# The opening of an encoder layer: the reciprocal root spread without a diagonal, `c` asked for first, chunk 0 by halves, the last squares summed apart, the sums of h held behind plain weights

## The chip, the core and the metric

The kernel runs on one core of a Trainium2 chip. A core has five engines that run their own instruction streams: TensorE (PE, whose weight loads are counted apart as PEld), VectorE (DVE), ScalarE (ACT), GpSimd (POOL) and SyncE (SP). DMA transfers are started from the queues of SP, ACT and POOL. The metric is the device time of one execution in microseconds; the time of a kernel is the median of its runs.

## What is computed

One layer of a bidirectional encoder, in float32, on 512 tokens of 1024 features. Its three blocks, a SwiGLU network, a pair of attention mixers and a second SwiGLU network, each read a normalised and modulated input, whose shift, scale and gate come from one vector `c`:

```python
c_act = silu(c)                                   # c (1024,)
mod = c_act @ w_mod + b_mod                       # w_mod (1024, 9 * 1024)
(sh1, sc1, g1, sh2, sc2, g2, sh3, sc3, g3) = split(mod, 9)

h = rmsnorm(x, norm_ffn1) * (1 + sc1) + sh1       # rmsnorm: x * rsqrt(mean(x*x, features) + EPS) * gain
x = x + 0.5 * g1 * swiglu(h, w_ffn1_in, w_ffn1_out)

h = rmsnorm(x, norm_mix) * (1 + sc2) + sh2        # then the two mixers, windowed and differential attention
x = x + g2 * (merged @ w_out)

h = rmsnorm(x, norm_ffn2) * (1 + sc3) + sh3
x = x + 0.5 * g3 * swiglu(h, w_ffn2_in, w_ffn2_out)
```

## The kernel before

Features lie on the 128 partitions, tokens on the free axis: `x` is eight tiles `x[0]` to `x[7]` of 128 features by 512 tokens, and "chunk k" is the features of `x[k]`. A product in float32 is made of three products of halves: a value is split into `high` (rounded by ACT) and `low` (value less high), and `w h` is taken as high·high + high·low + low·high. So each chunk of a weight matrix costs a load, a cast on ACT, a subtraction on DVE and three matmuls per output tile. `load_split` does it for the larger weights: line 211 loads `raw`, line 185 casts `high` on ACT, line 186 subtracts `low` on DVE; `mm3` (lines 174 to 176) issues the three matmuls.

A column of `mod` (128 features of a shift, scale or gate) is made by `mod_col`: a 128x1024 block of `w_mod` is loaded from SP's queue (512 KB), and DVE multiplies it with silu(c), which stands copied on all partitions, and sums along the row (line 272). For a scale, a second DVE operation on one column applies the norm's gain (line 279).

**The opening** stands in the order in which it is written (the scheduler leaves the order of all engines there):

1. ACT's queue loads `c` as one row, then `par` (all biases and gains); SP's queue loads `x[0]` to `x[7]`. Two matmuls of `ones` with the row spread `c` over the partitions (line 609). Eight filler matmuls on the identity follow (`warm`, line 615), whose output nobody reads.
2. SP's queue loads, for chunks 0 to 2, the scale's block, the first weights `w1s` (128x768) and the shift's block (`first_loads`).
3. The squares of `x` are taken on ACT, but on DVE for chunk 5, and added up on DVE (line 652). Eight matmuls with `ones` sum them over the features (line 337); DVE and POOL (line 308) make the reciprocal root, one value per token, tokens on partitions.
4. To have it along the free axis on every partition, DVE multiplies the identity with it to a `diagonal` (line 316), and a matmul of `ones` with the diagonal makes the `spread` (line 329). Fillers stand before and behind it.
5. The loop over the eight chunks. `hidden` makes chunk k of h: DVE x · scale · spread (line 346), ACT adds the shift and rounds `high` (line 347), ACT writes the value itself (line 350), DVE makes `low` (line 351). The weights of the chunk are split by `first_split` and `first_low`: for most chunks DVE subtracts (line 639), but for the chunks in `BY_DMA`, which are 1, 3, 5 and 7, ACT writes the negated high part (line 632) and a DMA of POOL's queue adds the weights to it in memory (line 633). Then 18 matmuls go into six banks (line 689):

```python
for w, h in ((wh, hh[k]), (wh, hl[k]), (wl, hh[k])):
    for i, out in enumerate(out1):
        PE.matmul(out, w[:, i * P : (i + 1) * P], h, start=first, stop=last)
```

**Behind the opening** three more rounds q = 3, 4, 5 of "plain" weights `w1i` follow, each with two weight blocks, 48 matmuls and `finish`; then the rest of the first network comes by "units", which multiply sums and differences of blocks of h with those of the weights. The sums and differences of h (`h_sum`: n1, n2, t3 and t4, each two operations on DVE at line 574 or 576 and two splits, lines 185 and 186) are made by calls that stand behind round 3 (n1, n2) and round 4 (t3, t4); here the scheduler places them on the engines by itself, as early as their operands allow.

**The two boundaries**, where `x` is complete and the next block's h is made, work by two halves of 256 tokens. Their order is written out too; each half takes its sums, root, diagonal and spread in the same way, while TensorE works on the other half's products. The call at the second boundary is at line 1762 and after; `x · scale · spread` is line 1717 there, and line 1123 is a transpose in the attention stage.

## Time and profile before

| | us |
|---|---|
| timed, median of 3 runs | 1063.11 |
| timed, lowest and highest | 1062.1, 1065.39 |
| the profiled execution, its own time | 1061.53 |
| the profiled execution, its span | 1059.8 |
| TensorE busy in the span | 1040.5 (98%) |
| DVE busy in the span | 794.8 (75%) |
| ACT busy in the span | 566.2 (53%) |
| mean granted TensorE clock | 0.997 of full speed |

The span runs from the first to the last recorded instruction; the rest of the execution's time, 1.7 us, lies around it. Rows of the profile give a line, an engine, an operation, `out<-in` by tile names, the shape, a count, and the busy time or the mean; a bracket like `[4.75 <-DVE sm L307]` says how long the engine had stood idle before the row and what ended that.

### The profile page before, as it was taken

What the parts mean: (1) busy time and instruction counts of PE and PEld (TensorE: products, weight loads), DVE (VectorE), ACT (ScalarE), POOL (GpSimd) and SP (SyncE); (2) the same over time, 40 slices, a digit from 0 to 9 for tenths busy, and PEclk for the clock granted to TensorE, in tenths of its full rate; (3) what the DMA queues carried; (4) which work ended last, traced back from release to release, by engine and by line L of the source; (5) the groups of instructions that cost most, each with busy time, mean ns of one, the idle gap of its engine ahead of it and who ended that gap; (6) DMA issues with size and microseconds to landing.
All of it is one profiled execution on the core that took longest, in us unless ns stands there. A gap on an engine that the chain in (4) does not pass through costs nothing.

```text
span 1059.8 us, 18652 instructions
## 1 busy us (share of the span) xinstructions
PE 1040.5 (98%) x7316; PEld 952.6 (90%) x7316; DVE 794.8 (75%) x1459; ACT 566.2 (53%) x928; POOL 154.9 (15%) x174
## 2 busy tenths in 40 slices
PE   7999999999999999999999999999999999999998
PEld 5789889899899998899778778989999999999997
DVE  7985667667796679859773587977889787867867
ACT  5564334344454352667765755534766546655553
POOL 1100010100110100443211101001111211112210
PEclk9999999999999999999999999999999999999999
DMA  9968687966974459695747843975498998988974
GB/s 340 365 208 201 209 212 190 265 158 203 281 184 152 165 199 410 217 269 126 180 92 186 225 148 101 371 224 118 97 232 195 222 230 215 222 221 214 214 151 125
DMA packets 69082, 220.91 MB, mean 208 GB/s; under 512 B 8193, under 2 KB 10881, under 8 KB 68994
## 3 DMA queue, kind: packets, MB, share of 16 engines
q1 hardware_dynamic: 46512, 146.52, 38.6%
q0 software_dynamic: 19488, 68.70, 35.2%
q10 hardware_dynamic: 2994, 4.51, 1.2%
q8 instruction: 57, 0.93, 0.3%
q14 instruction: 31, 0.25, 0.1%
HBM read 209.46 MB, written 10.23 MB: 207 GB/s over the span
## 4 chain that ended last, share of the span: by engine, by line
PE 78%; DVE 8%; issue 5%; ACT 5%; DMA 2%; POOL 1%; SPq 0%; ACTq 0%; DVEq 0%; POOLq 0%
PE acc L446 5%; PE acc L444 5%; PE acc L445 5%; PE sc L174 5%; PE sc L446 5%; PE sc L444 5%; PE sc L175 5%; PE sc L445 5%; PE sc L176 5%; PE acc L174 4%; PE acc L175 4%; PE acc L176 4%; PE acc L1045 2%; PE acc L1047 2%; PE acc L1046 2%
## 5 line engine op out<-in xcount | busy, mean ns | idle before, releaser
L185 ACT CAST high<-raw 128x1024 fp32r<-128x1024 f32 (+2 forms) x162 | 158.3, 986 | 166.6 <-PE acc L445 39.1
L186 DVE TENSOR_TENSOR low<-raw,high 128x1024 fp32r<-128x1024 f32 (+2 forms) x162 | 183.6, 1141 | 59.4 <-ACT high L185 58.5
L444 PE MATMUL acc<-b,high 128*128 128x256 f32 x508 | 141.0, 278 | 0.3 <-DVE f L523 0.3
L445 PE MATMUL acc<-b,high 128*128 128x256 f32 x508 | 140.6, 277 | 0.1
L446 PE MATMUL acc<-b,low 128*128 128x256 f32 x508 | 140.6, 277 | 0.0
L444 PE MATMUL sc<-b,high 128*128 128x256 f32 x500 | 138.4, 277 | 1.4 <-ACT f L521 1.4
L446 PE MATMUL sc<-b,low 128*128 128x256 f32 x500 | 138.5, 277 | 0.0
L445 PE MATMUL sc<-b,high 128*128 128x256 f32 x500 | 138.4, 277 | 0.0
L186 DVE TENSOR_TENSOR low<-u,high 128x1024 fp32r<-128x1024 f32 (+1 forms) x73 | 87.5, 1200 | 27.6 <-ACT high L185 26.2
L185 ACT CAST high<-u 128x1024 fp32r<-128x1024 f32 (+1 forms) x73 | 75.5, 1035 | 54.8 <-PE sc L175 16.0
L174 PE MATMUL sc<-b,high 128*128 128x512 f32 (+1 forms) x280 | 100.8, 360 | 0.0
L175 PE MATMUL sc<-b,high 128*128 128x512 f32 (+1 forms) x280 | 100.3, 358 | 0.0
L176 PE MATMUL sc<-b,low 128*128 128x512 f32 (+1 forms) x280 | 100.2, 358 | 0.0
L444 PEld LDWEIGHTS acc<-b,high 128*128 128x128 f32 x508 | 95.4, 188 | 0.8 <-DVE f L523 0.5
L445 PEld LDWEIGHTS acc<-b,high 128*128 128x128 f32 x508 | 95.5, 188 | 0.4 <-DVE b L1727 0.3
L446 PEld LDWEIGHTS acc<-b,low 128*128 128x128 f32 x508 | 95.4, 188 | 0.2 <-DVE low L186 0.2
L444 PEld LDWEIGHTS sc<-b,high 128*128 128x128 f32 x500 | 94.0, 188 | 1.6 <-ACT f L521 1.6
L446 PEld LDWEIGHTS sc<-b,low 128*128 128x128 f32 x500 | 93.9, 188 | 0.3 <-DVE low L186 0.2
L445 PEld LDWEIGHTS sc<-b,high 128*128 128x128 f32 x500 | 93.9, 188 | 0.0
L174 PE MATMUL acc<-b,high 128*128 128x512 f32 (+1 forms) x248 | 92.1, 371 | 0.2 <-DVE u L186 0.2
L176 PE MATMUL acc<-b,low 128*128 128x512 f32 (+1 forms) x248 | 90.2, 364 | 0.0
L175 PE MATMUL acc<-b,high 128*128 128x512 f32 (+1 forms) x248 | 90.1, 363 | 0.0
(369 smaller groups left out, 2675.4 us busy)
## 6 DMA issues: line engine op xcount, KB each, us to landing
u<-w_mod SPq DMA_DIRECT2D x40, 512.0 KB, 7.8
b<-w_mod SPq DMA_DIRECT2D x32, 512.0 KB, 6.0
raw<-w2i SPq DMA_DIRECT2D x31, 512.0 KB, 5.5
u<-w2i POOLq DMA_DIRECT2D x31, 512.0 KB, 7.0
u<-w1u POOLq DMA_DIRECT2D x24, 512.0 KB, 7.1
raw<-w1u SPq DMA_DIRECT2D x24, 512.0 KB, 6.8
raw<-w1o SPq DMA_DIRECT2D x24, 384.0 KB, 4.2
raw<-w_gate SPq DMA_DIRECT2D x16, 512.0 KB, 5.6
```

Of the source, the lines that this page charges most:

```text
L174: PE.matmul(out, wh, xh, start=first, stop=False)
L175: PE.matmul(out, wh, xl, start=False, stop=False)
L176: PE.matmul(out, wl, xh, start=False, stop=last)
L185: S.copy(hi, src)
L186: V.tensor_tensor(lo, src, f(hi), ALU.subtract)
L444: PE.matmul(out, wh[:, s], xh, start=first and j == 0, stop=False, skip_group_check=True)
L445: PE.matmul(out, wh[:, s], xl, start=False, stop=False, skip_group_check=True)
L446: PE.matmul(out, wl[:, s], xh, start=False, stop=last and j == 1, skip_group_check=True)
L1045: PE.matmul(out[t][:, 0:n], hh[k][:, ht], wh[:, o : o + n], start=k == 0, stop=False)
L1046: PE.matmul(out[t][:, 0:n], hh[k][:, ht], wl[:, o : o + n], start=False, stop=False)
L1047: PE.matmul(out[t][:, 0:n], hl[k][:, ht], wh[:, o : o + n], start=False, stop=k == NC - 1)
```

## The change

Nothing in the mathematics changes. In the opening:

- `c` is laid out as 128 rows of 8 values and is the first load of ACT's queue; eight matmuls of 128x128, the broadcast column with the identity, spread it over the partitions. The fillers are matmuls of 512 columns now: two before `c`'s, two behind, one on each of `x[4]`, `x[5]`, `x[6]`, one behind the sums and one behind the spread.
- All squares are taken on ACT. Chunk 7's are not added to the others but summed by a second group of eight matmuls into the same bank.
- `diagonal` is gone, here and at both boundaries. `spread` is one matmul for each 128 tokens, with the root's column, broadcast, as the weights and the identity as the moving operand. In the opening it stands behind the shift of chunk 0, and a small DVE copy of the root stands ahead of that.
- The shift's block of chunk 0 is loaded ahead of its weights `w1s`.
- Chunk 0 of h is made by halves of 256 tokens.
- The gain of the scale columns of chunks 1 to 7 is applied on ACT instead of at line 279 on DVE.
- Chunk 7 leaves `BY_DMA`; DVE makes its low weights in the loop's last turn.

Behind the opening, the plain weights of round q + 1 are asked for and split ahead of round q's products, behind the last splits issued before, and the sums of h are held (`issue_after`) behind splits of plain weights: n1 in round 3, the other three in round 5. `finish` is held in the same way.

The diff, with context cut; the tile `zero` of the attention stage, a small tile now, and the moved line of the tile `pos` are left out.

```diff
@@ -122,7 +122,7 @@
 LAST = 2
-BY_DMA = (1, 3, 5, 7)
+BY_DMA = (1, 3, 5)
@@ -182,10 +182,11 @@
     def split_from(hi, lo, src):
-        S.copy(hi, src)
-        V.tensor_tensor(lo, src, f(hi), ALU.subtract)
+        last = S.copy(hi, src), V.tensor_tensor(lo, src, f(hi), ALU.subtract)
+        split[:] = [i.ins for i in last]
+    split = []
     turn, holders = [0], {}
@@ -223,14 +224,8 @@
     make_identity(nc, ident)
-    crow = u4(F32).rearrange("p a b -> p (a b)")[0:1, :]
-    nc.scalar.dma_start(crow, a["c"].unsqueeze(0))
     par = keep([P, NPAR], "par")
     x = [xt() for _ in range(NC)]
-    nc.scalar.dma_start(par, a["par"])
-    for c in range(NC):
-        nc.sync.dma_start(x[c], a["x"][c])
@@ -264,7 +259,7 @@
         return begins[v]
-    def mod_col(v, c, w=None, in_order=False):
+    def mod_col(v, c, w=None, in_order=False, beside=False):
         if w is None:
@@ -276,7 +271,10 @@
             tc.keep_in_program_order(ins)
         if v in norms:
-            V.scalar_tensor_tensor(t, t, par[:, norms[v] + c : norms[v] + c + 1], b, ALU.mult, ALU.add)
+            if beside:
+                S.activation(t, t, AF.Identity, bias=b, scale=par[:, norms[v] + c : norms[v] + c + 1])
+            else:
+                V.scalar_tensor_tensor(t, t, par[:, norms[v] + c : norms[v] + c + 1], b, ALU.mult, ALU.add)
@@ -308,25 +306,16 @@
             return rs
-        def diagonal(self, rs, r=FULL[0]):
-            n = r.stop - r.start
-            nt = n // P
-            diag = f2()[:, 0:n]
-            V.tensor_tensor(
-                diag.rearrange("p (t q) -> p t q", t=nt),
-                ident.unsqueeze(1).broadcast_to([P, nt, P]),
-                rs.unsqueeze(2).broadcast_to([P, nt, P]),
-                ALU.mult,
-            )
-            return diag
-        def spread(self, diag, r=FULL[0]):
+        def spread(self, rs, r=FULL[0]):
...
             rb = self.st[r.start] if n < T else bank("op")
             rb = rb[:, T - n : T]
-            PE.matmul(rb, ones, diag, start=True, stop=True)
+            for t in range(n // P):
+                PE.matmul(
+                    rb[:, t * P : (t + 1) * P], rs[:, t : t + 1].broadcast_to([P, P]), ident,
+                    start=t == 0, stop=(t + 1) * P == n, skip_group_check=True,
+                )
             return rb
@@ -343,11 +332,17 @@
         t = f2()[:, r]
         s = modv[sh][:, c : c + 1]
+        if value is not None:
+            rb = rb[:, r]
         V.scalar_tensor_tensor(t, x[c][:, r], modv[sc][:, c : c + 1], rb, ALU.mult, ALU.mult)
...
         yield
         if value is not None:
-            S.activation(value, t.rearrange("p (t q) -> p t q", t=2), AF.Identity, bias=s)
+            if r.stop - r.start == T:
+                t3 = t.rearrange("p (t q) -> p t q", t=2)
+            else:
+                t3 = t.unsqueeze(1)
+            S.activation(value, t3, AF.Identity, bias=s)
         V.scalar_tensor_tensor(lo[:, r], t, s, f(hi[:, r]), ALU.add, ALU.subtract)
@@ -398,9 +393,9 @@
                     n += 1
                     if n == at[0]:
-                        diag = norm.diagonal(norm.close(ra), ra)
+                        rsa = norm.close(ra)
                     elif n == at[1]:
-                        ha = h_steps(norm.spread(diag, ra), ra)
+                        ha = h_steps(norm.spread(rsa, ra), ra)
                         run(ha, at[4])
@@ -408,10 +403,9 @@
             rs = norm.close(rb)
             run(ha, at[6])
-            diag = norm.diagonal(rs, rb)
             run(ha)
             run(steps, at[3])
-            hb = h_steps(norm.spread(diag, rb), rb)
+            hb = h_steps(norm.spread(rs, rb), rb)
             run(hb)
@@ -602,26 +596,41 @@
     cact = [sbuf("ka", [P, D], F32, 1)]
     hh, hl = new_h()
+    ccol = keep([P, 3 * NC], "ccol")[:, 0:NC]
+    nc.scalar.dma_start(ccol, a["c"])
+    tc.keep_in_program_order(nc.scalar.dma_start(par, a["par"]))
+    for c in range(NC):
+        nc.sync.dma_start(x[c], a["x"][c])
     with tc.manual_schedule(engines=BOUND | {mybir.EngineType.SP, mybir.EngineType.Pool}):
+        fill = bank("acc")
+        def warm(n, by=None):
+            if by is None:
+                by = ident.unsqueeze(1).broadcast_to([P, NT, P])
+            for i in range(n):
+                PE.matmul(fill, ident, by, start=True, stop=True)
+        warm(2)
         cb = [bank("sc") for i in range(2)]
-        for i in range(2):
-            PE.matmul(cb[i], ones[0:1, :], crow[:, i * T : (i + 1) * T], start=True, stop=True)
-        def warm(n):
-            out = bank("sc")[:, 0:P]
-            for i in range(n):
-                PE.matmul(out, ident, ident, start=True, stop=True)
-        warm(8)
-        w1 = {}
+        for n in range(NC):
+            i, j = n // 4, n % 4
+            PE.matmul(
+                cb[i][:, j * P : (j + 1) * P], ccol[:, n : n + 1].broadcast_to([P, P]), ident,
+                start=j == 0, stop=j == 3, skip_group_check=True,
+            )
+        warm(2)
+        w1, pos = {}, []
         def first_loads(k):
             scale = mod_load(SC1, k)
+            if k == 0:
+                pos.append(keep([P, NT], "pos", I32))
+            shift = mod_load(SH1, k) if k == 0 else None
             raw = sbuf("raw", [P, 1024], F32, RAW)
             nc.sync.dma_start(raw[:, 0:768], a["w1s"][k])
-            w1[k] = scale, mod_load(SH1, k), raw
+            w1[k] = scale, shift or mod_load(SH1, k), raw
@@ -644,24 +653,28 @@
         for c in range(NC):
             sq = f2()
-            if c == 5:
-                V.tensor_tensor(sq, x[c], x[c], ALU.mult)
-            else:
-                S.activation(sq, x[c], AF.Square)
-            if c:
+            S.activation(sq, x[c], AF.Square)
+            if c == NC - 1:
+                last = sq
+            elif c:
                 V.tensor_tensor(sq, sq, before, ALU.add)
...
                 for i in range(2):
                     S.activation(cact[0][:, i * T : (i + 1) * T], cb[i], AF.Silu)
-        n1.sums(sq, FULL[0], True, True)
+                warm(1, x[c + 1])
+            elif 4 < c < NC - 1:
+                warm(1, x[c])
+            if c == NC - 2:
+                n1.sums(sq, FULL[0], True, False)
+        n1.sums(last, FULL[0], False, True)
         mod_col(SC1, 0, w1[0][0])
         rs = n1.rstd(FULL[0])
-        warm(6)
-        diag = n1.diagonal(rs)
-        rb1 = n1.spread(diag)
-        warm(5)
+        warm(1)
+        V.tensor_copy(small(1), rs[:, 0:1])
         mod_col(SH1, 0, w1[0][1])
+        rb1 = n1.spread(rs)
+        warm(1)
         out1 = [b for _ in range(3) for b in pair_banks()]
@@ -670,18 +683,27 @@
                     hq[f"b{k // 4 + 1}{t + 1}"] = values[:, t * 1024 : (t + 1) * 1024]
                 values = values.rearrange("p (t k q) -> p t k q", t=2, k=4)
-            h1 = hidden(rb1, k, SC1, SH1, hh[k], hl[k], value=values[:, :, k % 4, :])
-            next(h1)
+            if k == 0:
+                h1 = [
+                    hidden(rb1, k, SC1, SH1, hh[k], hl[k], r, values[:, i : i + 1, k, :]) for i, r in enumerate(HALVES)
+                ]
+            else:
+                h1 = [hidden(rb1, k, SC1, SH1, hh[k], hl[k], value=values[:, :, k % 4, :])]
+            for h in h1:
+                next(h)
             if k + 3 < NC:
...
             if k == 0:
                 first_split(1)
+            elif k + 1 < NC:
+                mod_col(SC1, k + 1, w1[k + 1][0], beside=True)
+            for h in h1:
+                next(h)
+            if k == 0:
                 first_low(0)
-            elif k + 1 < NC:
-                mod_col(SC1, k + 1, w1[k + 1][0])
-            next(h1)
-            if k == 0:
-                mod_col(SC1, 1, w1[1][0])
+                mod_col(SC1, 1, w1[1][0], beside=True)
+            elif k == NC - 1:
+                first_low(k)
             wh, wl = w1.pop(k)[3:]
@@ -689,7 +711,8 @@
             if k + 1 < NC:
                 mod_col(SH1, k + 1, w1[k + 1][1])
-                first_low(k + 1)
+                if k + 2 < NC:
+                    first_low(k + 1)
             if k + 2 < NC:
@@ -835,22 +858,26 @@
         for q in range(3):
             finish(q, out1[2 * q : 2 * q + 2])
-        sums1 = ["n1", "n2", "t3", "t4"]
         units1 = {p: in_unit1(p) for p in range(PLAIN, NH)}
         for q in range(3, 2 * PLAIN):
-            w = loaded1 or [load_split(a["w1i"][q - 3, k], aside=ASIDE * (q == 5)) for k in range(2)]
-            loaded1 = None
+            w, sums_from = loaded1, split[1]
+            if q < 5:
+                with tc.issue_after(split[0]), tc.issue_after(split[1]):
+                    loaded1 = [load_split(a["w1i"][q - 2, k], aside=ASIDE * (q == 4)) for k in range(2)]
+            behind = split[1]
             out = pair_banks()
...
                     o = (k % 4) * 256 + i * P
                     mm3(out[i], wh[:, o : o + P], wl[:, o : o + P], hh[k], hl[k], k == 0, k == NC - 1)
-            for _ in range(2):
-                if sums1:
-                    h_sum(sums1.pop(0))
-            finish(q, out)
+            if q != 4:
+                with tc.issue_after(sums_from):
+                    for t in ("n1",) if q == 3 else ("n2", "t3", "t4"):
+                        h_sum(t)
+            with tc.issue_after(behind):
+                finish(q, out)
             if q == 3:
@@ -1759,10 +1786,10 @@
             if i == len(last) - 2:
                 run(steps, at[0])
-                diag = n3.diagonal(n3.close(T1), T1)
+                rsa = n3.close(T1)
             elif i == len(last) - 1:
                 run(steps, at[1])
-                ha = h_steps(n3.spread(diag, T1), 0)
+                ha = h_steps(n3.spread(rsa, T1), 0)
                 run(ha, at[4])
@@ -1773,11 +1800,10 @@
         for q in ("a12", "a22"):
             plain.prepare(q)
-        diag = n3.diagonal(rs, T2)
         run(ha)
         lead.prepare("a12")
         run(steps, at[3])
-        hb = h_steps(n3.spread(diag, T2), 1)
+        hb = h_steps(n3.spread(rs, T2), 1)
         run(hb, 3)
@@ -1880,7 +1906,7 @@
     o = {}
     o["x"] = con(n["x"].reshape(T, NC, P).transpose(1, 2, 0))
-    o["c"] = n["c"].reshape(D)
+    o["c"] = con(n["c"].reshape(NC, P).T)
     o["pos"] = con(n["positions"].reshape(NT, P).T)
```

More of the change, by code (lines that the diff above doesn't have):

```diff
@@ L700, in layer @@
     row = u4(F32).rearrange("p a b -> p (a b)")[:, 0:NROW]
-    pos = keep([P, NT], "pos", I32)
+    pos = pos[0]
     freq = keep([P, HD // 2], "freq")
@@ L1379, in start_a @@
         two = [v.rearrange("p (t k w d) -> p t k w d", t=NT, k=2, w=2) for v in two]
-        zero = keep([P, HD], "zero")
+        zero = small(1)
         V.memset(zero, 0.0)
```

## The prediction

> **What bounds the kernel now.** I read the page first, then busy time by stretches, then the chain of waits, then the timeline of the first 57 us.

> ```profile
> span 1059.8 us, 18652 instructions
> PE 1040.5 (98%) x7316; PEld 952.6 (90%) x7316; DVE 794.8 (75%) x1459; ACT 566.2 (53%) x928; POOL 154.9 (15%) x174
> ```

> TensorE is busy for 98% of the span. It idles for 1059.8 - 1040.5 = 19.3 us, and only that can be won. Stretches (columns: length, then busy time of PE, PEld, DVE, ACT, POOL, clock, DMA share, GB/s):

> ```profile
> 18.88:56.26 37.38, 34.94 (x145) 26.76 (x146) 37.17 (x64) 22.18 (x33) 4.35 (x5) 1.00 1.03 349
> 56.26:130.00 73.74, 73.74 (x444) 65.50 (x444) 50.09 (x68) 34.99 (x48) 6.06 (x7) 1.00 0.73 210
> ```

> From 18.88, where the first weight product starts, to 56.26, where the loop over the eight chunks has ended, DVE is busy for 37.17 of 37.38 us and the DMA engines are full. Afterwards TensorE has no idle time at all. So what the opening gains reaches the end, and the question is what the opening gains. Chain of waits (start, length, what):

> ```profile
> 17.99 0.95 DVE low L639
> ...
> 49.14 0.50 PE acc L689
> 49.63 0.23 PE sc L689
> ...
> 56.26 0.23 PE acc L174
> ```

> The chain runs along DVE from 18.0 until 49.1 (left out here: the same DVE lines over and over), then along 29 matmuls, (56.26 - 49.63)/29 = 0.228 us each. A chunk has 18 of them, 4.10 us; eight need 32.8 us, and the loop takes 37.4: 4.6 us are open to the change.

> **Ahead of the loop.**

> ```profile
> 1.02 0.29 POOL masks.py:199 TENSOR_SCALAR_AFFINE_SELECT ident<-ident 128x128 f32<-128x128 f32 x1
> 2.90 3.75 PE L609 MATMUL sc<-u,ones 1*128 1x512 f32 x4 [2.90 <-DMA u<-c]
> par<-par ACTq DMA_DIRECT2D x1, 48.5 KB, 3.2
> 6.58 3.55 PE L615 MATMUL sc<-ident 128*128 128x128 f32 x16
> 9.95 2.28 DVE L652 TENSOR_TENSOR f<-f,f 128x512 f32<-128x512 f32 x3
> 12.29 1.09 PE L337 MATMUL tp<-ones,f 128*128 128x2 f32 x8 [2.15 <-DVE f L652]
> 13.79 1.04 POOL L308 TENSOR_TENSOR sm<-sm,half 128x4 f32<-128x4 f32 x1 [4.75 <-DVE sm L307]
> 14.86 0.69 DVE L316 TENSOR_TENSOR f<-ident,sm 128x512 f32<-128x512 f32 x1 [1.16 <-POOL sm L308]
> 15.94 1.35 PE L329 MATMUL op<-f,ones 128*128 128x512 f32 x2
> 17.12 1.28 PE L615 MATMUL sc<-ident 128*128 128x128 f32 x10
> 17.32 0.75 DVE L346 SCALAR_TENSOR_TENSOR f<-x,mod,op 128x512 f32<-128x512 f32 x1 [0.57 <-PE op L329]
> 18.88 0.50 PE L689 MATMUL acc<-b,high 128*128 128x512 f32 x1 [0.48 <-ACT b L347]
> ```

> The sum of squares of chunk 5 moves from DVE to ACT and chunk 7's is no longer added. Two DVE operations go, and the last add ends near 10.6 instead of 12.2. But `c`, now in 128 short rows, lies behind two filler matmuls, and three more that read x stand ahead of the sums. `c` came at 2.9 in one row; `par`, of 128 rows, took 3.2 us. Asked for within the first microsecond, `c` is there between 2.9 and 4.2. The first two fillers need only the identity, which is done at 1.3; at half clock they last from 1.4 to 4.8 and hide `c`. The L615 rows show 8 and 5 matmuls as x16 and x10, two passes each; a 128-column pass takes 0.21 us at half clock (x16, less the end of the last) and 0.11 at full (x10). Seven 512-column matmuls (eight such passes each) and eight 128-column ones (two each) are 72 passes: 15.1 us at half clock, 7.9 at full. Full clock came here no later than the end of the first L615 run, 3.55 us after its start, since the sums behind it (x8) took 0.14 us a pass or less. So I take it between 1.4 + 3.4 = 4.8 and twice that time from the start, 8.2. The sums then start at 8.4 + half of that: 10.8 to 12.5. Two groups of sums of 0.9 us end at 12.6 to 14.3, against 13.4 now: nothing sure is won here.

> From there to the reciprocal root is the same 1.45 us (13.38 to 14.83). Then the diagonal's DVE operation (0.6) goes, the spread is four pairs of passes (0.9 at full clock) beside the shift column on DVE (1.3), and chunk 0 is made in halves (ACT can start on the first half when DVE has done at least half of the 0.75, so it is up to 0.3 earlier). The first product comes 2.75 us after the root instead of 4.05: at 16.8 to 18.5, from 18.88. Call it t0.

> **Inside the loop.**

> ```profile
> 26.06 0.95 DVE L639 TENSOR_TENSOR low<-raw,high 128x768 fp32r<-128x768 f32 x1
> 26.93 0.74 DVE L346 SCALAR_TENSOR_TENSOR f<-x,mod,op 128x512 f32<-128x512 f32 x1
> 27.59 1.21 DVE L272 CUSTOM_DVE_ANT_0 u<-u,ka 128x1024 f32<-128x1024 f32 x1
> 28.73 0.68 DVE L576 TENSOR_TENSOR b<-b 128x512 f32<-128x512 f32 x1
> 29.33 0.21 DVE L279 SCALAR_TENSOR_TENSOR mod<-mod,par,begin 128x1 f32<-128x1 f32 x1
> 29.46 0.74 DVE L351 SCALAR_TENSOR_TENSOR b<-f,mod,b 128x512 fp32r<-128x512 f32 x1
> 30.13 1.27 DVE L272 CUSTOM_DVE_ANT_0 u<-u,ka,par 128x1024 f32<-128x1024 f32 x1
> ```

> Start to start, one chunk costs DVE 0.66 + 1.14 + 0.66 + 1.20 = 3.66 us, and 0.87 more where DVE makes the low weights. Four operations of the sums of h (0.60 each, 2.4) leave the loop, and seven L279 (0.13 or more each, 0.9) go to ACT, which is busy for 22 of these 37 us. What is left on DVE is 4.10 us a chunk in the mean, as much as TensorE needs. By DVE alone the loop would end at t0 + 4.8 (from chunk 0 to chunk 1, below) + 7 x 4.10 = t0 + 33.5. Two other things end later.

> ```profile
> 20.61 0.91 POOL L633 DMA_DIRECT2D low<-w1s  x1 [5.78 <-ACT low L632]
> 23.69 0.50 PE L689 MATMUL acc<-b,high 128*128 128x512 f32 x1 [0.39 <-ACT b L347]
> 28.01 0.50 PE L689 MATMUL acc<-b,low 128*128 128x512 f32 x1 [1.30 <-DMA low<-w1s]
> 34.65 0.84 ACT L630 CAST high<-raw 128x768 fp32r<-128x768 f32 x1 [1.21 <-DMA raw<-w1s]
> 35.39 0.84 ACT L632 ACTIVATE low<-raw 128x768 fp32r<-128x768 f32 x1
> 36.52 0.86 POOL L633 DMA_DIRECT2D low<-w1s  x1 [9.63 <-ACT low L632]
> DMA to landing us min/median/max: 7.4/7.8/8.7
> ```

> Chunk 1's low weights are asked for 1.7 us after the first product and land 9.1 after it; TensorE wants them at about t0 + 7.6 (18.88 to 23.69 is 4.8 to chunk 1, then 12 matmuls) and stops for 1.3 us now. Everything in this moves with t0, so the stop stays and chunk 2 begins near t0 + 10.5.

> Chunk 5's low weights do not move with t0. ACT had waited until 34.65 for the raw weights, which lie in a stream that keeps the DMA engines full from the start; no byte ahead of them is taken away. So ACT is done at 36.2, the accumulating DMA is issued at 36.5 and lands 7.8 later, at 44.3. TensorE would want it at t0 + 10.5 + 3 x 4.10 + 2.7 = t0 + 25.5, at 42.3 to 44.0: earlier. It waits, and then has 6 + 18 + 18 = 42 matmuls, 9.6 us. The loop ends at 53.9 instead of 56.3: **2.4 us**, almost whatever t0 is. That chunk 7's transfer goes (DVE does it instead, 0.87, beside chunk 7's products) frees the stream only behind this point.

> [...]

> **Behind the loop.** All sums of h (sixteen such operations, at 0.60 each 9.6 us) now stand behind the splits of plain weights. On DVE, weight splits queue behind them, and TensorE's first unit waits for both; DVE's idle 73.74 - 50.09 = 23.7 us cover it. Without that cover up to 9.6 us of sums would stop TensorE. The two boundaries lose a diagonal per half:

> ```profile
> 740.45 0.42 DVE L316 TENSOR_TENSOR f<-ident,sm 128x256 f32<-128x256 f32 x1
> 740.78 0.47 DVE L1717 SCALAR_TENSOR_TENSOR b<-x,mod,tp 128x256 f32<-128x256 f32 x1
> 740.92 0.70 PE L329 MATMUL op<-f,ones 128*128 128x256 f32 x2 [0.50 <-DVE f L316]
> PE tp L1123 <- DVE u L186: 2.0, 5, 0.8
> ```

> At the second boundary the 0.50 goes, but the operations of h behind it, which TensorE waits for next, come only 0.33 earlier (740.45 to 740.78): 0.3 us won. At the first boundary no wait names the diagonal: nothing. The spread itself has as many passes as before. The built program also orders some transposes and products of the attention stage anew. The five waits at L1123 bound that: 2.0 us won to 2.0 lost. I take 0.

> **Sum.** 2.4 + 0.3 = 2.7 us: the profiled execution goes from 1061.53 to 1058.8. The timed runs are 1062.1, 1063.11 and 1065.39; the median of all four is 1062.6, so I expect 1059.9.

> **Rivals.** *The stream does not hold chunk 5* (0.23): if ACT gets the raw weights or the DMA lands 1.5 us sooner, the loop ends by chunk 1's stop, at t0 + 10.5 + 6 x 4.10 = t0 + 35.1, 51.9 to 53.6. At 52.5, in the middle, 3.8 us are won, with the boundary 4.1: 1058.5; where chunk 1's stop shrinks too (1.3), 1057.2. For it: landing ranges over 7.4 to 8.7, and with DVE ahead the stream may be asked for earlier. Against: it is full already.

> *Given back* (0.12): the attention stage's new order loses the 2.0 us, and the time is 1061.9, no measurable change. For it: five waits stand there now. Against: DVE has less to do.

> *The fillers run cold* (0.11, slower): if full clock does not come before the sums, these start at 1.4 + 15.1 = 16.5 and end at 20.0 (sixteen passes); 1.45 to the root, 1.7 for the spread at half clock and 1.4 to the first product put t0 at 24.5. Then chunk 5 is wanted at 50.0 and the loop ends at 59.6, 3.3 us later: 1065.6. It decides from t0 = 21.2, where t0 + 25.5 is 2.4 past 44.3. For it: the x16 row is cold although TensorE had been busy since 2.9. Against: that was one-row work (1x512), and 3.55 us of 128-row work ended it.
> [...]

> **How the numbers follow.** The forecast has 0.54, its own range 1058.5 to 1061.5. About 0.3% (3.2 us, below 1059.9) is what a measurement of this kernel can tell. Faster: the first rival and a little over half of the forecast, 0.54. Slower: the last rival and 0.01, 0.12. The rest, 0.34, is within. The range goes from 1056.2 (first rival with 1 of the 2.0 us won) to 1063.2.

> **What would show it.** Right: a second wait of TensorE for `low<-w1s`, between 42 and 44.3, the first product of plain weights near 53.9, and a spread at the second boundary that waits for nothing. Wrong: no such wait, or the loop ending before 52.5; TensorE stopping for sums of h between 75 and 100; passes of 0.21 us still at 12.

## The result: slower by 0.24%

The changed kernel takes 1066.21 us in the median of 13 runs (1063.56 to 1068.76), the kernel before 1063.11 us in 13 runs beside it. The ratio is 1.0024, with a 95% interval of 1.0012 to 1.0035. Forecast were 1059.9 us and a range that ended at 1063.2. One run of the experiments, of e3_wrap, was slow, 1733.55 us, and is counted in no figure below.

The profiled execution of the changed kernel took 1068.76 us, the slowest of its 13; sizes read from it may be too large, and the medians are used where a total is wanted. Its page:

```profile
span 1067.0 us, 18682 instructions
PE 1047.6 (98%) x7330; PEld 957.1 (90%) x7330; DVE 792.1 (74%) x1449; ACT 569.3 (53%) x937; POOL 154.0 (14%) x173
```

TensorE's idle time is 1067.0 - 1047.6 = 19.4 us, as before (19.3). What grew by 7 us is the time in which it counts as busy, and the page alone does not say where. So the same matmul was looked up in both traces, stage by stage, and the difference of its two start times taken (changed less before; each number is the difference of two rows):

| at (us, before) | stage | difference |
|---|---|---|
| 18.9 | first product of chunk 0 | -1.7 |
| 72 to 172 | plain weights, first units | -2.9 |
| 369 to 511 | first boundary, projections | -1.5 to -1.4 |
| 525 to 540 | gates and attention | between +4.9 and +7.0 |
| 566 to 735 | mixers, up to the second boundary | +4.7 to +5.0 |
| 768 to 805 | behind the second boundary | +6.1 |
| 834 to the end | second network | +6.7 |

The opening does what was forecast: it wins 2.9 us, and these reach 172 us untouched. 1.4 us go between 172 and 369 us; most of the loss, 6.2 us, is made between 511 and 525, in a stage whose text the diff does not touch. The three largest waits of TensorE in the changed kernel (us in total, times, longest):

```profile
PE acc L176 <- DMA low<-w_gate: 3.6, 1, 3.6
PE acc L711 <- ACT b L338: 1.5, 2, 0.8
PE tp L1150 <- DVE u L185: 1.4, 3, 0.9
```

The first line has no counterpart before: a product of a gate's weights waits 3.6 us for the low weights that a DMA of GpSimd adds up. Around it (columns as in the prediction's stretches; the third number from the end is the granted clock):

```profile
524.26:527.67 3.41, 1.24 (x6) 0.64 (x6) 2.17 (x9) 2.79 (x12) 0.00 (x0) 1.00 0.85 160
527.67:531.08 3.41, 1.97 (x5) 1.58 (x6) 1.39 (x4) 1.49 (x2) 1.97 (x2) 0.50 0.37 76
531.08:534.49 3.41, 3.41 (x10) 2.64 (x9) 0.00 (x0) 0.00 (x0) 0.00 (x0) 0.50 0.88 203
746.13:749.54 3.41, 1.89 (x14) 1.49 (x13) 2.12 (x5) 1.69 (x4) 0.00 (x0) 1.00 0.69 253
```

The wait, which ends at 529.1, is paid twice: while it lasts, and in half a clock that is granted for 6.8 us, from 527.7 to 534.5. A product of the gate takes 0.43 us from start to start there and 0.23 at full clock; 13 of them lose 2.6 us. That time is booked as busy. The wait itself is idle time: this stage (511 to 545 us before) has 2.9 us more of it and the opening 3.4 less, which is why the idle time did not grow. The last line belongs to the second boundary, below.

The opening itself, in the timeline of the changed kernel:

```profile
11.26 1.84 PE L326 MATMUL tp<-ones,f 128*128 128x2 f32 x16
13.40 1.04 POOL L306 TENSOR_TENSOR sm<-sm,half 128x4 f32<-128x4 f32 x1 [4.23 <-DVE sm L305]
14.49 1.16 PE L315 MATMUL op<-ident,sm 128*128 128x128 f32 x8 [0.42 <-POOL sm L306]
17.21 0.50 PE L711 MATMUL acc<-b,high 128*128 128x512 f32 x1 [0.70 <-ACT b L338]
26.28 0.50 PE L711 MATMUL acc<-b,low 128*128 128x512 f32 x1 [0.90 <-DMA low<-w1s]
43.51 0.50 PE L711 MATMUL acc<-b,low 128*128 128x512 f32 x1 [0.42 <-DMA low<-w1s]
53.18 0.39 PE L174 MATMUL acc<-b,high 128*128 128x512 f32 x1
```

Sums at 11.3, first product at 17.2, a stop for chunk 1's low weights, one for chunk 5's at 43.5, and the first product of plain weights at 53.2 (56.1 before).

### The profile page after: what moved, and what is told of

Same layout as the page of the kernel before. It is cut to its first block, busy times and chain, and to the rows that moved or that the text cites. A ratio compares the mean times of both kernels' runs of the same rounds, so it can differ in the third digit from the quotient of the medians.

```text
span 1067.0 us, 18682 instructions
## 1 busy us (share of the span) xinstructions
PE 1047.6 (98%) x7330; PEld 957.1 (90%) x7330; DVE 792.1 (74%) x1449; ACT 569.3 (53%) x937; POOL 154.0 (14%) x173
## 4 chain that ended last, share of the span: by engine, by line
PE 75%; issue 9%; DMA 5%; DVE 5%; ACT 4%; POOL 2%; ACTq 0%; POOLq 0%; DVEq 0%; SPq 0%
PE sc L174 5%; PE sc L176 5%; PE sc L175 5%; PE sc L438 5%; PE sc L440 5%; PE sc L439 4%; PE acc L176 4%; PE acc L174 4%; PE acc L175 4%; PE acc L438 4%; PE acc L440 4%; PE acc L439 4%; PE acc L1072 2%; PE acc L1074 2%; PE acc L1073 2%
## 5 line engine op out<-in xcount | busy, mean ns | idle before, releaser
L174 PE MATMUL sc<-b,high 128*128 128x512 f32 (+1 forms) x280 | 100.6, 359 | 0.0
L174 PE MATMUL acc<-b,high 128*128 128x512 f32 (+1 forms) x248 | 93.1, 376 | 0.0
```

The source lines that it names most:

```text
L174: PE.matmul(out, wh, xh, start=first, stop=False)
```

## Experiments: where the 6 us behind 500 us come from

In the built program the order of instructions differs from that of before in two places outside the edited code: matmuls 3191 to 3319 of TensorE (the gates and the attention, 518 to 542 us before) and 4177 to 4247 (the mixers' end, 680 to 689). Neither the opening, nor the boundaries, nor the holding of the sums moves them: with all of these in place, the program of e1_slot, below, has the old order. One line does, and e2_before_early_ask, where it alone is moved, has the new order in both places: the call that asks for round 5's plain weights now stands ahead of round 4's products, and so ahead of the preparation of the first unit's weights `s1`.

That call also takes a buffer. High and low weights live in five places of one long tile, handed out in turn by `high_low`, and a place held by a unit is skipped:

```python
i = turn[0] % HILO            # HILO = 5
turn[0] += 1
i = i * 1024 + aside          # aside: 0 to 64 columns
return tuple(t[:, i : i + n] for t in parts)
```

Before, `s1` got place 2 and round 5's weights 3 and 4; now the weights get 2 and 3 and `s1` gets 4. From the third place handed out after these on, every place is one lower (0 becomes 4) to the end of the kernel. The turn would not matter if the places were alike. They are not: weights that are set 16 columns `aside` reach 16 columns into the next place, and only place 4 has nothing behind it. In the attention stage gate 5 (j = 5) is set aside and gate 6 is not. Before, they had places 4 and 0, which share nothing. Now they have 3 and 4, which share 16 columns, and gate 6's split must wait until gate 5's products have been made. The transfers that add up the gates' low weights show it (line of the kernel before, then of the changed one, grouped between 470 and 530 us: count, issue in ns, start of the first and the last):

```profile
L986 POOL DMA_DIRECT2D low<-w_gate x6: 862/898/909, 476.8 to 522.9; - x6
```

```profile
L1013 POOL DMA_DIRECT2D low<-w_gate x6: 865/899/930, 475.6 to 529.6; - x6
```

The first, gate 5's, starts 1.2 us earlier than before, the sixth 6.7 us later. From gate 6 on, each comes one turn late: gate 6's starts at 498.6, where gate 7's started at 500.0 before, and gate 6's at 488.9.

Theory: this order of places costs the time. Rivals: the new opening, the held sums or the new spread make the later stages late.

**e1_slot**, the changed kernel with the places handed out as before:

```diff
+                if q == 4:
+                    slot = turn[0]
+                    turn[0] += 1
                 with tc.issue_after(split[0]), tc.issue_after(split[1]):
                     loaded1 = ...
...
+                later_slot, turn[0] = turn[0], slot
                 units1[PLAIN].prepare("s1")
+                turn[0] = later_slot
```

> The changed kernel with one thing taken back: round 5's plain weights are still asked for ahead of round 4's products, but the high and low buffers are handed out in the order of the kernel before. Theory (the order of the buffers costs the time): the opening's 2.9 us stay and all that was lost behind 100 us comes back, so about 1060.2, and TensorE's 3.6 us wait for low<-w_gate near 529 us is gone. Rival (something in the new opening, the held sums or the spread at the boundaries makes later stages late): as the changed kernel, about 1066.

Measured: 1059.74 us (12 runs), ratio to before 0.9971 [0.9959, 0.9982]. The wait for `low<-w_gate` is gone, and the attention stage has full clock:

```profile
500.00:560.00 60.00, 58.06 (x352) 46.47 (x351) 43.34 (x118) 44.49 (x103) 13.13 (x13) 1.00 0.57 139
```

The theory holds, the rivals fall: 6.5 us hang on the places that are handed out (by the two ratios 0.53%, 5.6 us).

**e2_before_early_ask**, the other way round: the kernel before with that call alone moved.

```diff
             loaded1 = None
+            if q == 4:
+                loaded1 = [load_split(a["w1i"][2, k], aside=ASIDE) for k in range(2)]
```

> The kernel before with one thing of the change alone: round 5's plain weights are asked for ahead of round 4's products, which moves the handing out of high and low buffers by one place for the rest of the kernel. Opening, sums of h and boundaries are as before. Theory: the whole later loss without the opening's gain, about 1069 (1066.2 + 2.9), with a wait of some 3 us for low<-w_gate near 525 to 530 us. Rival: no change, 1063.

Measured: 1070.63 us, ratio 1.0070 [1.0055, 1.0085]: 7.4 us lost without any of the opening. The same wait appears:

```profile
PE acc L176 <- DMA low<-w_gate: 3.8, 1, 3.8
```

**e3_wrap**, the changed kernel, places as changed, but gate 6 set aside too, so that the step from aside to not aside falls on the wrap from place 4 to place 0 again.

```diff
-            wh, wl = load_main(a["w_gate"][j], ASIDE * (j == EARLY_A))
+            wh, wl = load_main(a["w_gate"][j], ASIDE * (j in (EARLY_A, EARLY_A + 1)))
```

> The changed kernel, in which one more gate (j = 6 besides j = 5) has its weights set 16 columns aside. If what costs the time in the attention stage is that gate 5 (16 columns aside, buffer 3) and gate 6 (not aside, buffer 4) share 16 columns, so that gate 6's split must wait for gate 5's products, then this lifts it: about 4 to 6 us below the changed kernel, 1060.5 to 1062, and no wait for low<-w_gate near 529 us. If the addresses alone matter, or the opening, about 1066.

Measured: 1060.93 us (11 runs), ratio 0.9977 [0.9967, 0.9988]. The attention stage's order is that of before again, and there is no wait for `low<-w_gate`. 5.3 of the 6.5 us are back; the rest, 1.2 us, lies within the two intervals.

**e9_before_gate5_not_aside**, the kernel before with gate 5 moved by 16 columns and nothing else:

```diff
-            wh, wl = load_main(a["w_gate"][j], ASIDE * (j == EARLY_A))
+            wh, wl = load_main(a["w_gate"][j], 0)
```

> The kernel before with one thing changed: gate 5's weights are not set 16 columns aside, so that they share 16 columns with the last weights of the projections ahead (buffer 3, aside) instead of beginning at the wrap from buffer 4 to buffer 0. Nothing else moves, no buffer is handed out in another order. Theory (16 shared columns make a split wait for the products of the buffer beside it, and the loads of the attention stage then come one turn late): slower by 3 to 7 us, 1066 to 1070, with waits of TensorE for low<-w_gate between 470 and 550 us. Rival (the turn of the buffers as such, or their addresses, cost the time): 1062.5 to 1063.5.

Measured: 1072.42 us, ratio 1.0081 [1.0068, 1.0093]: 9.1 us lost, more than expected.

```profile
PE acc L176 <- DMA low<-w_gate: 2.5, 1, 2.5
PE acc L174 <- ACT high L984: 1.5, 1, 1.5
```

No place is handed out in another order here, and no opening is new. Sixteen shared columns are enough.

## Experiments: what each part is worth

**e4_free_sums**: the changed kernel with the block of plain weights and sums of h of the kernel before.

```diff
-            w, sums_from = loaded1, split[1]
-            if q < 5:
-                with tc.issue_after(split[0]), tc.issue_after(split[1]):
-                    loaded1 = ...
+            w = loaded1 or [load_split(a["w1i"][q - 3, k], aside=ASIDE * (q == 5)) for k in range(2)]
+            loaded1 = None
...
+            for _ in range(2):
+                if sums1:
+                    h_sum(sums1.pop(0))
+            finish(q, out)
```

> The changed kernel with the plain weights and the sums of h as in the kernel before (not held, asked for in their own rounds); opening and boundaries changed. The buffers then are those of before too. Theory: no later loss, but four operations of the sums, 2.4 us of VectorE, back in the loop: 1060.5 to 1062.6, loop over the chunks ending up to 2.4 us later than the changed kernel's 53.35. If the held sums give nothing because the loop is held by something else: 1060.2, loop end at 53.4. Rival (opening or boundaries cause the loss): 1066.

Measured: 1062.43 us, ratio 0.9991 [0.9981, 1.0002]. The loop ends at 53.9, only 0.7 behind the changed kernel. Three operations of the sums, not four, stand in it (at 35.4, 47.3 and 47.9), and they cost it little: the profiles of e1_slot, e3_wrap and e8_diagonals, which have the changed kernel's opening and loop, end it between 52.7 and 53.8. But then:

```profile
66.03 0.50 PE L174 MATMUL acc<-b,high 128*128 128x512 f32 x1 [1.11 <-ACT high L185]
```

Round 4's weights come 1.1 us late, and between 62 and 68 us 1.9 more are lost against the changed kernel. The loop had ended 2.2 us sooner than before, and its next reader was not ready: most of the opening's gain is given back here unless the weights are asked for a round ahead.

**e5_sums_free_early_ask**: e1_slot with the weights asked for ahead, but the sums not held.

```diff
-            if q != 4:
-                with tc.issue_after(sums_from):
-                    for t in ("n1",) if q == 3 else ("n2", "t3", "t4"):
-                        h_sum(t)
+            if q < 5:
+                for t in ("n1", "n2") if q == 3 else ("t3", "t4"):
+                    h_sum(t)
```

> As e1_slot, but the four sums of h are not held: n1 and n2 stand behind round 3 and t3 and t4 behind round 4 as before, and the scheduler puts four of their operations back into the loop over the chunks. The plain weights are still asked for one round ahead. If what the block of plain weights gains over e4_free_sums (2.7 us) is VectorE's relief in the loop, as the prediction had it, this gives it up: 1061.5 to 1062.5. If it is the weights asked for early (in e4_free_sums TensorE waits 1.1 us at 66.0 for the cast of round 4's weights), it keeps it: 1059.5 to 1060.3.

Measured: 1067.46 us, ratio 1.0040 [1.0026, 1.0055]. Neither expectation. Up to 91 us it runs 0.3 to 0.4 us behind e1_slot, loop end 53.0: the three operations of the sums in the loop cost nothing that could be told. Then the first unit's weights are late. SP's queue, which loads them, waits for a column of `mod` (line 267) that stands on VectorE behind the sums, 23.5 us against 13.2 in e1_slot, and the loads go out ten us later (e1_slot, then e5_sums_free_early_ask):

```profile
66.16 0.38 SPq L472 DMA_DIRECT2D raw<-w1u  x1
76.60 0.38 SPq L472 DMA_DIRECT2D raw<-w1u  x1
```

ScalarE then sits idle for 7.7 us, until 92.4, for a transfer of these weights, and TensorE stops:

```profile
94.93 0.58 PE L438 MATMUL tp<-b,high 128*128 128x256 f32 x1 [3.27 <-ACT high L185]
96.50 0.58 PE L440 MATMUL tp<-b,low 128*128 128x256 f32 x1 [0.77 <-DVE low L185]
```

4.0 us of waits, and half a clock granted from 94.2 to 101.0. Asking early without holding the sums loses more than it gains (holding them without asking early was not run), and what the holding saves is at 95 us, not in the loop.

**e6_block_alone**: the kernel before with that block (asked early, sums held, places as before). Its diff is the block's part of the change, with e1_slot's lines.

> The kernel before with the block of plain weights alone (asked for one round ahead, sums of h held), buffers handed out in the order of before; opening and boundaries as before. If the loop is bound by VectorE, four operations less (2.4 us) end it near 54 in place of 56.3, and this has most of the gain without a new opening: about 1061. If opening and block only pay together, 1062.8 to 1063.5.

Measured: 1060.89 us, ratio 0.9986 [0.9973, 0.9998]. With the old opening four operations less on VectorE do end the loop earlier, at 54.4 for 56.1. From its first product it lasts 35.4 us; in the three profiles with the old loop and sums (before, e2_before_early_ask, e9_before_gate5_not_aside) it lasts 37.2.

**e11_loop_with_old_head**: e6_block_alone, and in the loop line 279 on ScalarE for chunks 1 to 7 and chunk 7 out of `BY_DMA`.

```diff
-BY_DMA = (1, 3, 5, 7)
+BY_DMA = (1, 3, 5)
...
-                mod_col(SC1, k + 1, w1[k + 1][0])
+                mod_col(SC1, k + 1, w1[k + 1][0], beside=True)
```

> As e6_block_alone (opening ahead of the loop as before: fillers, c as a row, diagonal, chunk 0 whole), with the change's loop: line 279 on ScalarE for chunks 1 to 7 and chunk 7's low weights by VectorE. The prediction said that the loop ends near 53.9 almost whatever the start of the first product is, held by chunk 5's transfer. Then about 1060, near e1_slot. If TensorE's own pace from the first product holds it (18.9 + 32.8 + stops of 2.3 = 54.0 to 54.5), it is 0.7 to 1.4 behind e1_slot: 1060.4 to 1061.1.

Measured: 1061.52 us, ratio 0.9983 [0.9969, 0.9997]; first product at 19.46, loop end at 55.3. No wait for chunk 5's low weights shows; the loop ends some 36 us behind the first product, with 2.3 us of stop for chunk 1's. The loop's own changes gain nothing here: e6_block_alone, without them, ended it at 54.4.

**e12_l279_on_vector**: e1_slot without `beside=True`.

> As e1_slot, but the gain of the scale columns is applied on VectorE (line 279) again. By the prediction's sum that puts 0.9 us back on VectorE in the loop: if VectorE binds there, 1060.3 to 1060.7; if TensorE's pace does, 1059.5 to 1060.0.

Measured: 1059.96 us, ratio 0.9965 [0.9953, 0.9977]. Moving line 279 to ScalarE is worth nothing that can be measured.

**e7_dma_1_3** and **e10_dma_3**: e1_slot with `BY_DMA = (1, 3)` and with `BY_DMA = (3,)`.

> As e1_slot, but chunk 5's low weights too are made by VectorE and not by the accumulating DMA. The prediction held that this transfer ends the loop; then the wait for low<-w1s near 43.5 goes and VectorE's rate takes over (0.87 more): loop end within 0.5 of e1_slot's 52.8 on either side, 1059.2 to 1060.3. If VectorE has no room in the loop, its 0.87 and more shows as waits for b<-f L351 or low<-raw: 1060.6 or more.

> As e1_slot, but VectorE makes the low weights of chunks 1 and 5 too; only chunk 3's come by the accumulating DMA. TensorE's stop for chunk 1's low weights (1.3 us near 26.7 in e7_dma_1_3) goes. If VectorE has the time: 1058.3 to 1058.8. If not, its 0.87 more ahead of chunk 1 or 2 shows as a longer wait for b<-f L351 or ACT b, and it is 1059.5 or more.

Measured: 1059.55 us, 0.9966 [0.9954, 0.9979], and 1061.31 us, 0.9979 [0.9969, 0.9989]. Without chunk 5's transfer there is no wait at 43.5, and 52.7 is the loop's end. e1_slot, with the transfer, does not wait for it either and ends at 52.7 too; where it waits (0.42 us in the changed kernel, 0.45 in e3_wrap and e8_diagonals), it holds the loop by no more than that. Without chunk 1's, its stop goes, but VectorE is late for chunk 1 instead (ACT waits for it, then TensorE: 1.65 for 0.78 in e7_dma_1_3), and the loop ends at 53.9:

```profile
23.79 0.50 PE L711 MATMUL acc<-b,high 128*128 128x512 f32 x1 [1.65 <-ACT b L338]
```

**e8_diagonals**: e1_slot with the diagonal back at both boundaries.

```diff
-        hb = h_steps(n3.spread(rs, T2), 1)
+        diag = n3.diagonal(rs, T2)
...
+        hb = h_steps(n3.spread_d(diag, T2), 1)
```

> As e1_slot, but both boundaries make the spread by the diagonal again, as before; the opening stays changed. The prediction gave the boundaries 0.3 us: 1060.0, and in the trace the spread of the second boundary waits 0.5 us for the diagonal again, with the two waits behind it (0.76 and 0.76 in e1_slot) shorter by 0.1 to 0.5. If the diagonal had cost nothing: 1059.7.

Measured: 1060.19 us, ratio 0.9969 [0.9956, 0.9981]: not to be told from e1_slot by time. In the trace the 0.5 us wait of the spread is back and costs 0.35 at that place, close to the 0.3 of the prediction.

The opening with the boundaries (e4_free_sums) gives 0.09%, not clear of zero, the block alone (e6_block_alone) 0.14%, all together (e1_slot) 0.29%; by the intervals this is not to be told from their sum. e1_slot, e7_dma_1_3 and e12_l279_on_vector beat both kernels, by 0.29 to 0.35% the kernel before, and cannot be told from each other.

## Why the prediction was wrong, and where it was right

**The step that failed** is the last one behind the loop: "The built program also orders some transposes and products of the attention stage anew. The five waits at L1123 bound that: 2.0 us won to 2.0 lost. I take 0." The new order was seen and not explained. It was bounded by the waits that stood there before, as if another order could only shift those. But it was the trace of a new dependence, and its price was that of a transfer issued too late, 3.6 us in one profile, plus 2.6 us at the half clock that stood behind it. The rival that named it ("given back") carried the same 2.0 us. The sum without that step was 1059.9 us; the kernel without that cause took 1059.74. That these agree so closely is partly luck: the gain in the loop came in another way than forecast.

The cause of that cause was in the diff. The prediction followed the earlier call of the loads past the sums and the splits on each engine; it did not follow it past `prepare("s1")`, which draws on the same turn of buffers.

**Ahead of the loop**: right. Full clock came at 5.4 us (4.8 to 8.2 forecast), the sums began at 11.3 (10.8 to 12.5 forecast), the first product at 17.2 (16.8 to 18.5). The 3.4 us in that range, and their doubling, were the author's estimate, and no run shows them: full clock came 4.1 us behind the first filler here, and in the kernel before at 9.76, 3.2 behind the first filler of line 615. Not seen was that the clock before had fallen back to half from 13.2 to 16.6 us, across the root and the start of the spread; the changed opening keeps full clock there.

**Inside the loop**: the size was right, 2.9 us for 2.4, the mechanism only in part. Chunk 5's second wait came where it was forecast (43.51 in a stretch of 42 to 44.3), with 0.42 us, but it does not fix the end of the loop: in e1_slot, with the latest first product of the four profiles with this opening and loop (17.9), the transfer has landed in time and the loop ends first, at 52.7. What holds the loop once it starts at 17 is TensorE itself, 32.8 us, and 2.0 to 3.7 us of stops, most of them for the h and the low weights of chunk 1. The stop for these low weights, which the prediction left at 1.3, was 0.2 to 1.4 in profiles of the same code. The first rival, "the stream does not hold chunk 5", was nearer. That the sums of h bind the loop fits the old opening (e6_block_alone, 1.7 us earlier) and not the new (e5_sums_free_early_ask, with three of the four operations back).

**What is late next** was not asked for the loop's end. "Afterwards TensorE has no idle time at all. So what the opening gains reaches the end" holds only because the change also asks for round 4's weights earlier; e4_free_sums shows the 1.9 us that go otherwise. The prediction costed the early call at nothing and gave it no gain. The cover of the sums, VectorE's idle time, is not what decides: in e5_sums_free_early_ask VectorE idles for 6.6 us ahead of 83.3 and 7.2 ahead of 93.5, and TensorE still waits 4.0, because the sums stand ahead of the operation that lets the next loads go. Their place counts, not only their length.

**The boundaries**: 0.3 forecast; 0.35 by the traces of e1_slot and e8_diagonals, but in four of the eight profiles without the diagonal a drop of the clock behind it costs 1.6, which the prediction did not see (last section). **The fillers** did not stay cold: passes of 128 columns began 0.21 us apart up to 5.4 us and 0.11 apart from 5.5 on.

Two stretches of the changed kernel that looked like further losses do not seem to belong to the change: a wait of 0.7 us at 247.5 and matmuls slower by 4% from 306 to 323 (0.118 us from start to start, for 0.113 in the kernel before). e7_dma_1_3, which has the places of before, shows the wait too (0.76 at 246.6) and falls 1.9 us behind e1_slot between 186 and 327; e2_before_early_ask and e9_before_gate5_not_aside, with the old opening and sums, show the wait as well (0.8). So no run ties the wait to the change; what made the matmuls slower was not shown.

## What to carry to other kernels

A load that is asked for earlier also takes its buffer earlier; where buffers go round in turn, every later user moves by a place, so each call that draws on the same turn must be followed through to the end of the kernel, above all where places are not alike. When the order of instructions changes in a stage that the edit does not touch, the dependence that made it change has to be found before it is priced; the waits that stand there now are no bound for it. And a stage that ends sooner is worth only what its next reader can take: look at when that reader's operands come.

## What the runs showed of the hardware

That the clock fell to half after so little idle time was not expected. At the second boundary of e1_slot TensorE waits 0.76 us twice, the two waits ending 1.3 us apart, and then:

```profile
737.28:740.69 3.41, 1.89 (x14) 1.49 (x13) 2.44 (x4) 1.69 (x4) 0.00 (x0) 1.00 0.56 203
740.69:744.10 3.41, 3.41 (x18) 3.41 (x18) 2.06 (x5) 3.34 (x7) 0.00 (x0) 0.50 0.44 144
```

In the 3.41 us ahead of the drop TensorE was busy for 1.89, more than half, and still got half the clock for the next 3.41, which cost 1.6 us (the lead over the kernel before falls from 5.04 to 3.48 us across it). e4_free_sums, with the same two waits, keeps full clock:

```profile
739.24:742.65 3.41, 2.99 (x26) 2.79 (x25) 2.44 (x5) 1.92 (x4) 0.00 (x0) 1.00 0.60 177
742.65:746.07 3.42, 2.31 (x17) 2.11 (x18) 2.37 (x5) 1.70 (x4) 0.00 (x0) 1.00 0.63 184
```

```profile
741.50:744.91 3.41, 1.89 (x14) 1.48 (x13) 2.36 (x4) 1.72 (x3) 0.00 (x0) 1.00 0.63 245
```

In these traces, what tells the windows apart is how many products they hold. Count a product of 512 columns and 128 rows as one, a smaller one by its share of columns and of rows; at full clock, 0.228 us each, 15 fill a window. Behind 18 us, the 14 traces have some 4200 windows at full clock with 7 or more, and all of them kept it (the fewest 7.5 in the kernel before and 8 in the changed one); all with 6 or fewer lost it (1.75 to 6 at the eight drops inside the kernels), but for one of 5.5 in the last 7 us of e8_diagonals. At the second boundary, 3.41 us at full clock can be laid so that they hold only 5.5 products without the diagonal, and no fewer than 7 with it, where the waits are about 0.5, 0.3 and 0.76 and lie further apart. Accordingly, of the eight profiles without the diagonal at the boundaries four show this drop (5.5 to 6 products in the window), of the six with it none. So taking the diagonal away wins 0.35 us there and, when the windows fall badly, costs 1.6. The count is read from these traces and was not tested by a run of its own; by time e8_diagonals and e1_slot are alike.
